# DeltaNet level: joining 32x32 block inverses with float32 products in place of zero-padded float16 operands

## The chip, the cores and the metric

The kernel runs on one core of one Trainium2 chip. Times are device microseconds of one execution of the whole program. The time before is 3229.03 us, the median of three runs (3227.76 to 3230.68). A profile is one execution of its own: the one read here took 3223.55 us, and its span from the first to the last instruction is 3221.8 us.

## The reference, cut to what matters

The layer normalises its input (two sequences of 4096 and 2048 rows, 1024 wide), projects it once, and runs three head groups on the projection: windowed attention, a gated DeltaNet in both directions of time, and cross-attention to a memory. Their gated outputs go through one output projection and a second layer norm. The part that the change touches is the triangular solve inside the DeltaNet, done for chunks of 64 rows, per head and per direction:

```python
a = jnp.einsum('...id,...jd->...ij', k_beta, k) * decay
def solve(rhs):
    return lax.linalg.triangular_solve(a, rhs, left_side=True, lower=True, unit_diagonal=True)
u = solve(v * beta[..., None])
w = solve(k_beta * jnp.exp(g)[..., None])
```

The unit triangular 64x64 matrix of a chunk is inverted by blocks. With the inverses A and B of its two 32x32 diagonal blocks and the 32x32 block N that lies off the diagonal, the missing block of the inverse is the product of three: A, N and B, with a sign. Joining the two inverses by these two small products is what the kernel calls a level.

## The kernel before, in words

A tile is 128 rows of a sequence, so it holds two chunks; there are 48 tiles and four DeltaNet heads. The program has three stages one after another. The first normalises, projects, convolves and does the windowed attention. The second goes forward over the 24 pairs of tiles: DeltaNet in the forward direction, with the gate projections and the memory attention (`gate_mem`, L1661) of the tiles as other work beside it. The third goes backward over the pairs: DeltaNet in the other direction, with the output projection and the last layer norm (`finish`, L1750) beside it. The loop of the second and third stage is `pipe` (L1705).

DeltaNet has these steps for each tile. `dn_front` (L1435) builds the decayed key products `n` for two pairs of tiles at a time and inverts their 32x32 diagonal blocks on GpSimd (`dn_invert`, L916: buffers `na`, `nb`, `tb`, with round trips through DRAM); the inverses come back as the tile `uc`, 128 partitions by 4 heads by 32 columns of float32. `dn_back` (L1455) then calls `dn_level` (L966), which joins the inverses to 64x64 ones in `th`, and `dn_chain` (L1011), which carries the state from tile to tile; its products with `th` (`psx`) and with `n` (`psb`) are float32 products of 64x64 blocks already.

The level before works with float16 pairs. `split` (L808) writes a float32 value as a high part (ScalarE, a copy to float16) and a low part (VectorE, the remainder), and `mm3` (L839) multiplies two such pairs with three matmuls. For a level `uc` is split into `tc_`, and VectorE transposes both parts in blocks of 32x32 into `tt`. The off-diagonal blocks of `n`, one for each of the two chunks (q = 0, 1), are split into `n64h` and `n64l`. These two, and `yth` and `ytl` for the second product, are 128x128 operands per head that are zero outside the two blocks; they exist once for the whole program (`dn_alloc`, L854) and were set to zero at the start of stages two and three (`dn_static`, L858). So each product handles all 128 partitions, and one matmul does both chunks.

The order of the instructions is not that of the code. Every call is recorded, and a planner (`schedule`, L342, and `order`, L268) simulates the engines with an estimated cost per instruction (`full_cost`, L137) and issues all of them in the order that it finds (`flush`, L500). On that account the profile puts nearly every instruction on L505, and instructions are told apart by the names of the tiles. For the PE the planner counts a matmul of n columns as the larger of 25 ns and n/2.4 ns plus 2.5 ns, four times that for float32. Each engine then runs its own list strictly in that order. The PSUM tiles of the level (`psy`, `psz`) share two buffers with the output of the chain (`pso`, tag "dn").

Of the kernel before, what the change touches and what calls it, by code (L numbers as in the profile page):

```python
# [9 lines left out]
F32 = mybir.dt.float32  # L10
F16 = mybir.dt.float16
BF16 = mybir.dt.bfloat16
I32 = mybir.dt.int32
AF = mybir.ActivationFunctionType
# [5 lines left out]
P = 128  # L20
# [530 lines left out]
def encoder(ctx: ExitStack, tc: tile.TileContext, A, outs):  # L551
    nc = tc.nc
    plan = Plan(tc)
    V, S, G, T, Q = plan.engines()
# [253 lines left out]
    def split(eng_hi, dst_h, dst_l, src, scale=None):  # L808

        if scale is None:  # L810
            S.activation(dst_h, src, AF.Copy)
            V.tensor_tensor(dst_l, src, dst_h, op=ALU.subtract)
        else:
            S.activation(dst_h, src, AF.Copy, scale=scale)
            V.scalar_tensor_tensor(dst_l, src, scale, dst_h, op0=ALU.mult, op1=ALU.subtract)
# [23 lines left out]
    def mm3(out, stat, mov, start=True, stop=True):  # L839

        T.matmul(out, lhsT=stat[0], rhs=mov[0], start=start, stop=False)
        T.matmul(out, lhsT=stat[0], rhs=mov[1], start=False, stop=False)
        T.matmul(out, lhsT=stat[1], rhs=mov[0], start=False, stop=stop)
# [3 lines left out]
    YB = 1  # L847
    NAB = 1
    KSB = 1
    dstat = {}  # L850
    for nm in ("n64h", "n64l", "yth", "ytl"):
        dstat[nm, 0] = [P, 4, 128]

    def dn_alloc(pool):  # L854
        for (nm, pr), shp in list(dstat.items()):
            dstat[nm, pr] = pool.tile(shp, F16, name=f"{nm}{pr}", tag=f"{nm}{pr}", bufs=1)

    def dn_static(dr):  # L858
        for s_ in dstat.values():
            V.memset(s_, 0.0)  # L860

    def features(pool, t, tag):
        fm = pool.tile([P, 8, P], F16, tag=tag, name=tag, bufs=2)
        Q.dma_start_transpose(out=fm, in_=dst_d[t].rearrange("p h t s d -> p (h t s d)"))
        return fm
# [100 lines left out]
    def dn_level(pool, psp, dr, d):  # L966

        uc, n = d["uc"], d["n"]
        i0, i1 = (0, 1) if dr == 0 else (1, 0)
        nn = n.rearrange("q h (b c) -> q h b c", b=4)  # L970
        tc_ = pool.tile([P, 2, 4, 32], F16, tag="tc", name="tc_", bufs=2)
        split(None, tc_[:, 0], tc_[:, 1], uc)
        tt = pool.tile([P, 2, 4, 32], F16, tag="tt", name="tt", bufs=2)
        V.transpose(tt.rearrange("p a h c -> p (a h c)"), tc_.rearrange("p a h c -> p (a h c)"))
        n64 = (dstat["n64h", 0], dstat["n64l", 0])
        for q in range(2):
            r = slice(64 * q + 32 * i0, 64 * q + 32 * i0 + 32)
            c = slice(64 * q + 32 * i1, 64 * q + 32 * i1 + 32)
            split(None, n64[0][r, :, c], n64[1][r, :, c], nn[r, :, 2 * q + i1])
        psy = psp.tile([P, 512], F32, tag="dn", name="psy")  # L980
        py = psy[:, 0:128].rearrange("p (h c) -> p h c", h=4)
        for h in range(4):
            mm3(py[:, h], (n64[0][:, h], n64[1][:, h]), (tt[:, 0, h], tt[:, 1, h]))
        yt = (dstat["yth", 0], dstat["ytl", 0])
        for q in range(2):
            r = slice(64 * q + 32 * i1, 64 * q + 32 * i1 + 32)
            c = slice(64 * q + 32 * i0, 64 * q + 32 * i0 + 32)
            split(None, yt[0][r, :, c], yt[1][r, :, c], py[r])
        psz = psp.tile([P, 512], F32, tag="dn", name="psz")
        pz = psz[:, 0:128].rearrange("p (h c) -> p h c", h=4)  # L990
        for h in range(4):
            mm3(pz[:, h], (yt[0][:, h], yt[1][:, h]), (tc_[:, 0, h], tc_[:, 1, h]))
        th = pool.tile([P, 4, 64], F32, tag="th", name="th", bufs=2)
        S.activation(th[:, :, 0:32], uc, AF.Copy, scale=rowA)
        S.activation(th[:, :, 32:64], uc, AF.Copy, scale=rowB)
        for q in range(2):
            r = slice(64 * q + 32 * i0, 64 * q + 32 * i0 + 32)
            c = slice(32 * i1, 32 * i1 + 32)
            S.activation(th[r, :, c], pz[r], AF.Copy)
        d["th"] = th  # L1000

    state = {}
# [452 lines left out]
    def dn_back(pool, psp, dr, tiles, ds, emit_out):  # L1455
        for i, (t, d) in enumerate(zip(tiles, ds)):
            dn_level(pool, psp, dr, d)
            first = pos_of[t] == 0 if dr == 0 else pos_of[t] == lens[seq_of[t]] - 1
            if first:
                dn_reset(pool)  # L1460
            emit_out(t, *dn_chain(pool, psp, dr, d))
# [137 lines left out]
    pn = p23.enter_context(plan.pool(name="pn", bufs=1))  # L1599
    pd2 = p23.enter_context(plan.pool(name="pd2", bufs=2, space=PSUM))  # L1600
    pb = p23.enter_context(plan.pool(name="pb", bufs=1, side="right"))
    dn_alloc(pn)
    dn_static(0)
    vmts = {}

    def memory(t):
# [129 lines left out]
            Q.dma_start(out=w[:, c:c + 2], in_=wo_d[:, 4 * i + c:4 * i + c + 2])  # L1736
    Q.dma_start(out=grow, in_=A["ln_g"][0].partition_broadcast(P))
    Q.dma_start(out=brow, in_=A["ln_b"][0].partition_broadcast(P))
    dn_static(1)
    osum = {}  # L1740

    def out_b(t, po, eg):
# [74 lines left out]
```

## Time and profile before

| | |
|---|---|
| median of three runs | 3229.03 us |
| the profiled execution, its span | 3223.55 us, 3221.8 us |
| PE busy | 2833.5 us, 88% of the span |
| PE weight loads busy | 1889.5 us, 59% |
| VectorE (DVE) busy | 2652.9 us, 82% |
| ScalarE (ACT) busy | 2179.3 us, 68% |
| GpSimd (POOL) busy | 1765.8 us, 55% |

A busy share is the part of the span in which the engine had an instruction in it. Matmuls overlap each other in the array, so their durations (0.38 us for one of 512 columns) are longer than the distance at which they follow each other, and the distance is what a matmul costs the PE. The rows on which the prediction rests stand further down.

### The profile page before, as it was taken

How to read it: one execution, taken by the hardware profiler on the slowest of the kernel's cores; microseconds unless marked ns; L12 is line 12 of the kernel's file. 1: busy time of each engine (PE TensorE's matmuls, PEld its weight loads, DVE VectorE, ACT ScalarE, POOL GpSimd, SP SyncE). 2: the span in 40 equal slices, each digit the busy share in tenths (PEclk: the TensorE clock that was granted, in tenths of full speed). 3: DMA queues.
4: the chain of work that ended last, by engine and by line, in shares of the span. 5: the costliest groups of instructions: out<-in, count | busy, mean ns of one | idle time of the engine just before them, and what ended most of it. 6: DMA issues, size and time to landing. Idle time of an engine off the chain costs nothing.

```text
span 3221.8 us, 79556 instructions
## 1 busy us (share of the span) xinstructions
PE 2833.5 (88%) x28704; PEld 1889.5 (59%) x28704; DVE 2652.9 (82%) x6256; ACT 2179.3 (68%) x5623; POOL 1765.8 (55%) x2923
## 2 busy tenths in 40 slices
PE   5789887888988897778999999999998998898998
PEld 4666766667666675445565555665554554554544
DVE  8799877899999999678878787887778887887875
ACT  5677756777777776577777667776666666565543
POOL 5756444455565455535734253444538766867762
PEclk9899988999999998889999999999999999999999
DMA  7999999999999999899888887877798887777763
GB/s 220 260 228 233 221 225 229 240 236 214 228 210 226 207 227 254 206 224 197 189 182 203 188 200 160 174 175 164 159 218 209 195 189 183 190 185 178 187 170 114
DMA packets 1336900, 652.35 MB, mean 202 GB/s; under 512 B 1127728, under 2 KB 1261744, under 8 KB 1332280
## 3 DMA queue, kind: packets, MB, share of 16 engines
q1 hardware_dynamic: 1336504, 647.27, 87.5%
q8 instruction: 225, 3.69, 0.5%
q14 instruction: 171, 1.40, 0.1%
HBM read 227.54 MB, written 175.19 MB: 125 GB/s over the span
## 4 chain that ended last, share of the span: by engine, by line
PE 24%; DVE 24%; POOL 19%; DMA 13%; issue 8%; ACT 8%; SPq 3%; POOLq 0%; ACTq 0%; DVEq 0%
PE psg L505 8%; POOL nb L505 6%; POOL tb L505 5%; DVE acc L505 5%; PE pso L505 4%; PE psf L505 3%; SPq L505 3%; DMA apt<-aphl 3%; DVE lg L505 2%; DVE aphl L505 2%; PE psk L505 2%; DMA na<-nd 2%; PE psx L505 1%; ACT lg L505 1%; DMA uc<-ud 1%
## 5 line engine op out<-in xcount | busy, mean ns | idle before, releaser
L505 PEld LDWEIGHTS <-xT 128*128 128x128 f16 x5760 | 535.7, 99 | 381.4 <-issue 43.8
L505 PE MATMUL psf<-xT,w1f 128*128 128x256 f16 (+1 forms) x3600 | 443.2, 276 | 13.3 <-DVE vtm L505 7.8
L505 PE MATMUL psg<-w2a,xT 128*128 128x512 f16 (+1 forms) x2304 | 435.5, 330 | 6.4 <-DVE qtm L505 4.4
L505 PEld LDWEIGHTS <-w1f 128*128 128x128 f16 x3600 | 341.0, 101 | 56.6 <-DVE vtm L505 7.2
L505 POOL TENSOR_TENSOR nb<-nb,tb 128x30 f32<-128x30 f32 (+6 forms) x750 | 342.7, 457 | 48.7
L505 POOL TENSOR_TENSOR tb<-nb,na 128x30 f32<-128x30 f32 (+6 forms) x750 | 327.0, 436 | 48.4
L505 DVE SCALAR_TENSOR_TENSOR acc<-cb,cw,acc 128x256 f32<-128x256 f32 x576 | 326.1, 598 | 7.3 <-POOL cb L505 4.6
L505 ACT ACTIVATE lg<-lg,mx,scal 128x385 f32<-128x385 f32 (+1 forms) x384 | 263.8, 688 | 89.7 <-DVE mx L505 81.6
L505 PEld LDWEIGHTS <-yT 128*128 128x128 f16 x2304 | 201.2, 98 | 193.2 <-issue 9.9
L505 PE MATMUL pso<-w2b,yT 128*128 128x512 f16 x1152 | 297.4, 385 | 0.0
L505 PE MATMUL pso<-w2a,yT 128*128 128x512 f16 x1152 | 291.5, 381 | 1.4 <-DMA yT<-yhl 1.4
L505 PE MATMUL pslg<-kfm,qfm 128*128 128x128 f16 x2240 | 197.3, 230 | 108.3 <-DVE mx L505 105.1
L505 PEld LDWEIGHTS <-qfm 128*128 128x128 f16 x2624 | 201.4, 102 | 154.3 <-issue 127.3
L505 PE MATMUL psg<-w2b,xT 128*128 128x512 f16 x1152 | 290.2, 384 | 0.0
L505 PE MATMUL psq<-w1t,xT 128*128 128x512 f16 x1152 | 283.2, 383 | 2.5 <-ACT cb L505 2.5
L505 POOL TENSOR_TENSOR x<-x,grow 128x256 f32<-128x256 f32 x208 | 189.1, 925 | 128.9 <-ACT x L505 117.4
L505 DVE TENSOR_TENSOR aphl<-lg,aphl 128x768 f16<-128x768 f32 (+1 forms) x192 | 201.5, 1049 | 56.2 <-ACT aphl L505 56.0
L505 POOL TENSOR_TENSOR n<-raw 128x256 f32<-128x256 f16 x96 | 79.6, 840 | 245.6 <-DMA raw<-cfh 113.1
L505 DVE CUSTOM_DVE_ANT_0 lg<-pslg,bias 128x385 f32<-128x385 f32 (+1 forms) x384 | 195.2, 540 | 22.8 <-ACT oat L505 10.8
L505 POOL TENSOR_TENSOR x<-x,brow 128x256 f32<-128x256 f32 x208 | 193.9, 949 | 0.0
L505 ACT ACTIVATE aphl<-lg 128x768 f16<-128x768 f32 (+1 forms) x192 | 156.4, 815 | 17.8 <-DMA apt<-aphl 15.9
L505 PE MATMUL psk<-w1t,xT 128*128 128x272 f16 x1152 | 157.9, 284 | 9.3 <-DVE qktm L505 9.2
(921 smaller groups left out, 6865.9 us busy)
## 6 DMA issues: line engine op xcount, KB each, us to landing
x<-x SPq DMA_DIRECT2D x48, 512.0 KB, 4.0
xT<-xT SPq DMA_DIRECT2D x24, 1024.0 KB, 5.8
xT<-xT SPq DMA_DIRECT2D x48, 512.0 KB, 4.7
r<-x SPq DMA_DIRECT2D x48, 512.0 KB, 4.1
out_dram<-r SPq DMA_DIRECT2D x48, 512.0 KB, 3.7
cr<-crow SPq DMA_DIRECT2D x47, 512.0 KB, 4.8
yhl<-yhl SPq DMA_DIRECT2D x48, 384.0 KB, 3.2
x<-in_x_prompt_dram SPq DMA_DIRECT2D x32, 512.0 KB, 4.9
```

The lines of the kernel that those rows point to most:

```text
L505: getattr(self.eng[o["e"]], o["name"])(*o["args"], **o["kw"])
```

## The change

The level takes its operands as they are, in float32, and multiplies the 32x32 blocks where they lie. There is no split of `uc`, of `n` or of the intermediate product, and there are no operands padded with zeros. Each product is now one matmul per head and per chunk, on 32 partitions, in place of three per head on 128 partitions. The transpose reads `uc` itself (float32, 128 columns, where it was float16, 256 columns). The intermediate product goes from PSUM to the tile `yt` by ScalarE as float32; `yt` has two buffers where `yth` and `ytl` had one. The last copies into `th` are the same as before.

```diff
-    dstat = {}
-    for nm in ("n64h", "n64l", "yth", "ytl"):
-        dstat[nm, 0] = [P, 4, 128]
-    def dn_alloc(pool):
...
-    def dn_static(dr):
-        for s_ in dstat.values():
-            V.memset(s_, 0.0)
...
-        tc_ = pool.tile([P, 2, 4, 32], F16, tag="tc", name="tc_", bufs=2)
-        split(None, tc_[:, 0], tc_[:, 1], uc)
-        tt = pool.tile([P, 2, 4, 32], F16, tag="tt", name="tt", bufs=2)
-        V.transpose(tt.rearrange("p a h c -> p (a h c)"), tc_.rearrange("p a h c -> p (a h c)"))
-        n64 = (dstat["n64h", 0], dstat["n64l", 0])
-        for q in range(2):
-            r = slice(64 * q + 32 * i0, 64 * q + 32 * i0 + 32)
-            c = slice(64 * q + 32 * i1, 64 * q + 32 * i1 + 32)
-            split(None, n64[0][r, :, c], n64[1][r, :, c], nn[r, :, 2 * q + i1])
+        tt = pool.tile([P, 4, 32], F32, tag="tt", name="tt", bufs=2)
+        V.transpose(tt.rearrange("p h c -> p (h c)"), uc.rearrange("p h c -> p (h c)"))
+        rows = [[slice(64 * q + 32 * i, 64 * q + 32 * i + 32) for q in range(2)] for i in (i0, i1)]
         psy = psp.tile([P, 512], F32, tag="dn", name="psy")
         py = psy[:, 0:128].rearrange("p (h c) -> p h c", h=4)
         for h in range(4):
-            mm3(py[:, h], (n64[0][:, h], n64[1][:, h]), (tt[:, 0, h], tt[:, 1, h]))
-        yt = (dstat["yth", 0], dstat["ytl", 0])
+            for q in range(2):
+                T.matmul(py[rows[1][q], h], lhsT=nn[rows[0][q], h, 2 * q + i1], rhs=tt[rows[0][q], h],
+                         start=True, stop=True)
+        yt = pool.tile([P, 4, 32], F32, tag="yt", name="yt", bufs=2)
         for q in range(2):
-            r = slice(64 * q + 32 * i1, 64 * q + 32 * i1 + 32)
-            c = slice(64 * q + 32 * i0, 64 * q + 32 * i0 + 32)
-            split(None, yt[0][r, :, c], yt[1][r, :, c], py[r])
+            S.activation(yt[rows[1][q]], py[rows[1][q]], AF.Copy)
         psz = psp.tile([P, 512], F32, tag="dn", name="psz")
         pz = psz[:, 0:128].rearrange("p (h c) -> p h c", h=4)
         for h in range(4):
-            mm3(pz[:, h], (yt[0][:, h], yt[1][:, h]), (tc_[:, 0, h], tc_[:, 1, h]))
+            for q in range(2):
+                T.matmul(pz[rows[0][q], h], lhsT=yt[rows[1][q], h], rhs=uc[rows[1][q], h], start=True, stop=True)
...
-    dn_alloc(pn)
-    dn_static(0)
...
-    dn_static(1)
```

## Rows read from the trace of the kernel before

**Rows 1.** The page, its first part: busy time, share, instructions.
```profile
PE 2833.5 (88%) x28704; PEld 1889.5 (59%) x28704; DVE 2652.9 (82%) x6256; ACT 2179.3 (68%) x5623; POOL 1765.8 (55%) x2923
```

**Rows 2.** Busy time by stage: stretch, length, engines, granted clock, DMA share, GB/s.
```profile
0.00:1380.00 1380.00, 1147.77 (x12288) 880.25 (x12288) 1192.66 (x2834) 971.41 (x2287) 734.68 (x903) 0.94 1.00 227
1380.00:2322.00 942.00, 871.75 (x8989) 554.27 (x8990) 761.57 (x1813) 687.88 (x1900) 437.60 (x956) 0.97 0.83 186
2322.00:3222.00 900.00, 814.01 (x7429) 455.01 (x7426) 698.66 (x1610) 520.03 (x1437) 593.53 (x1065) 0.98 0.75 182
```

**Rows 3.** The chain that ended last, 3150 to 3222 us: start, length, what.
```profile
3181.19 31.34 PE pso L505 x155
```

**Rows 4.** Waits of the PE, 1380 to 3222 us: total us, times, longest.
```profile
PE psx L505 <- DVE v L505: 27.0, 41, 1.9
PE psy L505 <- DVE tt L505: 26.4, 12, 5.8
PE psr L505 <- DVE shl L505: 16.1, 23, 2.0
PE psy L505 <- DVE of L505: 10.6, 8, 2.1
...
PE psk L505 <- DVE p L505: 7.6, 7, 3.2
PE psr L505 <- ACT shl L505: 6.2, 8, 2.0
...
PE psz L505 <- DVE ytl L505: 2.1, 4, 0.8
```

**Rows 5.** Groups of PE instructions by shape, 1380 to 3222 us: count, busy, mean ns.
```profile
L505 PE MATMUL psx<-v,th 64*64 64x64 f32 x1536 | 132.3, 226 | 31.8 <-DVE v L505 27.0 <-DVE ost L505 2.2 <-ACT th L505 0.9
...
L505 PE MATMUL psy<-tt,n64h 128*128 128x32 f16 x768 | 44.7, 178 | 37.6 <-DVE tt L505 26.4 <-DVE of L505 10.6 <-DVE ofs L505 0.3
```

**Rows 6.** The PE in order of time: start, length to the last end, what.
```profile
1594.91 0.68 PE L505 MATMUL psx<-v,th 64*64 64x64 f32 x8
1595.51 0.21 PE L505 MATMUL psy<-tt,n64h 128*128 128x32 f16 x2
...
1595.83 1.02 PE L505 MATMUL psg<-w2a,xT 128*128 128x512 f16 x4
1596.78 0.68 PE L505 MATMUL psb<-v,n 64*64 64x64 f32 x8
...
1598.57 0.68 PE L505 MATMUL psx<-v,th 64*64 64x64 f32 x8
1599.18 0.21 PE L505 MATMUL psz<-tc__22114,yth 128*128 128x32 f16 x2
...
1599.49 1.67 PE L505 MATMUL psg<-w2b,xT 128*128 128x512 f16 x7
1601.00 0.19 PE L505 MATMUL pss<-rx,kc 128*128 128x64 f16 x1
```

**Rows 7.** The tile psx: ns shortest, median, longest; first and last start.
```profile
L505 PE MATMUL psx<-v,th x1536: 218/218/366, 1410.3 to 3181.0; 64*64 64x64 f32 x192
```

**Rows 8.** Tiles n64h, n64l, ytl, tt, uc: ns shortest, median, longest.
```profile
L505 ACT ACTIVATE n64h<-n x192: 292/306/311, 1380.9 to 3158.2; 32x128 f16<-32x128 f32 x192
L505 DVE TENSOR_TENSOR n64l<-n,n64h x192: 236/287/716, 1383.0 to 3159.2; 32x128 f16<-32x128 f32 x192
L505 DVE TENSOR_TENSOR ytl<-psy,yth x192: 268/286/299, 1394.0 to 3170.4; 32x128 f16<-32x128 f32 x192
L505 DVE STREAM_TRANSPOSE tt<-tc__21583 x1: 388/388/388, 1381.2 to 1381.2; 128x256 f16<-128x256 f16 x1
L505 DVE STREAM_TRANSPOSE tt<-tc__26088 x1: 430/430/430, 3152.1 to 3152.1; 128x256 f16<-128x256 f16 x1
L505 ACT ACTIVATE tc__21583<-uc x1: 310/310/310, 1380.4 to 1380.4; 128x128 f16<-128x128 f32 x1
L505 DVE TENSOR_TENSOR tc__21583<-uc,tc__21583 x1: 292/292/292, 1380.8 to 1380.8; 128x128 f16<-128x128 f32 x1
```

More of the change, by code (lines that the diff above doesn't have):

```diff
@@ L849, in encoder @@
     KSB = 1
-    dstat = {}
-    for nm in ("n64h", "n64l", "yth", "ytl"):
-        dstat[nm, 0] = [P, 4, 128]
-    def dn_alloc(pool):
-        for (nm, pr), shp in list(dstat.items()):
-            dstat[nm, pr] = pool.tile(shp, F16, name=f"{nm}{pr}", tag=f"{nm}{pr}", bufs=1)
-    def dn_static(dr):
-        for s_ in dstat.values():
-            V.memset(s_, 0.0)
     def features(pool, t, tag):
@@ L995, in dn_level @@
         S.activation(th[:, :, 32:64], uc, AF.Copy, scale=rowB)
[L996 to L999, printed above, removed]
+        for r in rows[0]:
+            S.activation(th[r, :, 32 * i1:32 * i1 + 32], pz[r], AF.Copy)
         d["th"] = th
```

## The prediction

> **What bounds the kernel now.** I read the busy shares first, then the same by stage, then the chain that ended last, then what the PE waits for, and last the PE instruction by instruction around a level. The reader is to see that the PE is the fullest engine of the whole program [rows 1], and that in the two stages which run levels (1380 to 2322 us forward, 2322 to 3222 us backward) it is busy 871.75 of 942 and 814.01 of 900 us, against 761.57 and 698.66 us for VectorE and 687.88 and 520.03 us for ScalarE [rows 2]. The PE's idle time there is 70 + 86 = 156 us in 1842. The granted clock is 0.97 and 0.98, so it is nearly always at the 2.4 GHz level and a level has little to win or lose there. How the kernel ends says the same: the longest piece of the last chain is 31.34 us of output-projection matmuls back to back, 155 of them [rows 3]. The recurrence is over by then and the PE is working off a backlog, so what the levels add to the PE's list comes out at the end, unless the PE idles less elsewhere. So the change is a trade: dearer or cheaper PE work, against PE stalls that other engines cause. The first stage holds no level and stays as it is.
>
> **The price of a product on the PE now.** Distances between starts count, not durations. The 12 float16 matmuls of `psy` start at 1595.51 and the next group at 1595.83: 0.32 us, 0.027 us each. Those of `psz` take 1599.18 to 1599.49, 0.31 us [rows 6]. They are of the same shape as the gate matmuls around them, and nothing is lost at either side. There are 96 levels with two products each, 192 products at 0.315 us.
>
> **The price of a float32 group.** The chain's `psx` and `psb` are four calls of 64x64 blocks each and show as 8 records; the 1536 records of `psx` are two for each of 96 x 2 x 4 calls [rows 5]. So one float32 matmul is two records, and a product of the changed level (4 heads x 2 chunks) is 16 records of 32 columns. What surrounds such a group: seven gate matmuls fill 1599.49 to 1601.00, 0.216 us each; the four ahead of `psb` should take 0.864 us from 1595.83, but `psb` starts after 0.95 us, so entering costs 0.09 us. The group's length is 0.68 us to its last end [rows 6], and one record takes 0.218 us [rows 7]; the last starts 0.46 us after the first, 0.066 us apart. From there to the next group's start (1595.51) it is 0.14 us, 0.07 more than a distance. So a group costs 0.16 us for changing over, and 0.066 us a record of 64 columns.
>
> A rule of the Trainium skill speaks against the change at this place: "TensorEngine Tiling (Array Packing)", Tiling Modes, Key Properties, says that going from one tiling of the array to another drains it. The trace agrees as far as it goes, with the 0.09 and 0.07 us above. By the rule each of the 192 products pays this, and by the rows as well.
>
> A record of 32 columns in float32 stands in no row. Bounds: not below the 0.027 us of the float16 matmuls of 32 columns if the array takes one after the other; not above the 0.066 us of the 64-column record, if the cost doesn't fall with the columns. Half the latter, 0.033 us, is what columns alone would give, it is near the lower row, and I take it. Then a product costs 16 x 0.033 + 0.16 = 0.69 us, 0.375 us more than now, and 192 of them 72 us. With 0.027 us it is 53 us, with 0.066 us 173 us. Below that lies only the case in which the two chunks of a head run at the same time (first rival): half of 0.033 us a record, 21 us.
>
> **What the other engines lose.** VectorE: 192 `n64l` at 0.287 us (55 us), 192 `ytl` at 0.286 us (55 us), 96 low parts of `uc` at 0.292 us (28 us); 138 us. The transposes take 0.388 to 0.430 us for 256 float16 columns [rows 8]; for 128 float32 columns I allow from the same down to half, so 0 to 20 us saved, and take 10. The eight memsets are under 3 us. In all about 148 us of the 1460 us that VectorE is busy in the two stages. ScalarE: 192 `n64h` at 0.306 us and 96 high parts at 0.310 us [rows 8], 89 us of 1208; the copies to `yth` remain as copies to `yt`. None of this counts by itself, as neither engine sets the end; it counts where the PE waits for them.
>
> **What the PE stalls lose.** `psy` waited 26.4 us for `tt` [rows 4]. Today `uc` passes ScalarE, VectorE, VectorE before the matmul, and every hop queues behind other work; afterwards the transpose reads `uc` directly. I take back 20 of the 26.4 us, and the 2.1 us for which `psz` waited for `ytl`. The 10.6 us in which `psy` waited for `of`, the reader of the output in PSUM, stay: `psy`, `psz` and `pso` still share two buffers. The chain's own waits for VectorE and ScalarE (`psx` for `v` 27.0, `psr` for `shl` 16.1 and 6.2, `psk` for `p` 7.6: 57 us [rows 4]) get shorter, because these engines' queues are emptier: VectorE's idle share goes from 0.21 to (1842 - 1312)/1842 = 0.29, more by two fifths. I take a third, 19 us, an estimate; the bounds are none and all of the 57 us, since an operand that is late by its own chain stays late. Together 41 us, between 15 and 86.
>
> What is late next: `yt` now comes by ScalarE alone, and the PE meets it or waits for it as it does for `yth`; the level's last copies into `th` are unchanged, so `psx` still queues behind them. The added PE work delays what stands behind it in the PE's list, gate and output matmuls for the most part, which nothing waits for soon. The planner counts the new matmuls at 100 ns a call by its formula, 0.8 us a product, close to my 0.69 us, so it will leave room for them; but all else is put in a new order too, and that moves single waits either way.
>
> **Sum.** 72 - 41 = 31 us more: 3223.55 + 31 = 3254.6 us for an execution like the profiled one. The median of the runs shown stands 5.5 us above it, so 3260 us. The chance I give this case, slower with records near half price, is 0.50; its own range is 3240 to 3295.
>
> **Rivals.**
> 1. The two chunks of a head overlap in the array. They lie on other rows and other columns of it (partitions 0 to 63 and 64 to 127) and alternate in the issue. The direct cost is then 21 us and the net 21 - 41 = -20 us: 3209 us. It decides from a record distance of 0.02 us down: there 16 x 0.02 + 0.16 - 0.315 = 0.165 us a product, 32 us in all, and the 41 us outweigh it by more than 6.5 us. For it: nothing else would use the idle quarters of the array. Against it: no float32 rows in the trace come closer than 0.066 us, though all of those sit on one and the same block of the array. Chance 0.17. The Trainium skill has this rule in "TensorE: Matmul & The Clock Gate", Part 3, Packing small matmuls: matmuls in different row and column groups start a few ns apart. "TensorEngine Tiling (Array Packing)", Gotcha 1, speaks against it here, since row tiles may not be in one PSUM bank at the same time and both chunks write into `psy`. No run here shows either.
> 2. The emptier queues of VectorE and ScalarE are worth more than I take: with nearly all of the 86 us, and 12 more from waits too small to be listed, 72 - 98 = -26 us, 3203 us. For it: over half of the PE's 156 us of idle time ends with one of these two engines. Against it: an engine with a fifth of its time free makes others wait mostly by order, not by load. Chance 0.12.
> 3. A record costs as much with 32 columns as with 64: 173 - 41 = +132 us, 3361 us. For it: the weight load ahead of each record may be what sets the 0.066 us, and it might have a fixed part. Chance 0.12.
> 4. It evens out: direct cost at its lower bound of 53 us, stalls shrinking by about 53 us. Within 0.2% (6.5 us), about what a measurement of this kernel can tell from no change. Chance 0.09.
>
> **How the numbers follow.** The predicted time is that of the likeliest case, 3260 us. Slower by over 0.2%: 0.50 + 0.12 = 0.62. Faster by over 0.2%: 0.17 + 0.12 = 0.29. Within: 0.09. The range 3198 to 3330 us takes in the likeliest case, the first, second and fourth rival's times, and the third's up to a record distance of some 0.055 us; about 0.1 is left above it and 0.07 below.
>
> **What would show it.** In the profile after: `psy` and `psz` as 16 float32 records of 32x32 each, 3072 in all, with a group taking about 0.6 us to the next start and 0.09 us lost ahead of it; under 0.4 us means the first rival, over 1.1 us the third. VectorE busy about 148 us less and ScalarE 89 us less, all after 1380 us. The row of `psy` waiting for `tt` down to some 6 us. The backlog of output matmuls at the end as long as now or longer. The prediction is wrong if the PE's idle time in the two stages falls by more than the groups add, or if the first stage's length changes.

## The result, and the profile after

The changed kernel takes 3318.73 us (median of four runs, 3312.04 to 3322.77) against 3228.4 us for the kernel before: a ratio of 1.0279, 95% interval 1.0257 to 1.0300. It is slower by 90 us. The forecast was slower by 31 us; the range, to 3330 us, holds the time, but the size is three times what was forecast.

The page's first part after, which answers to [rows 1]:

```profile
PE 2918.9 (88%) x29472; PEld 1912.9 (58%) x29472; DVE 2504.9 (76%) x5768; ACT 2100.1 (63%) x5335; POOL 1741.8 (53%) x2923
```

VectorE is busy 148 us less, just as forecast, ScalarE 79 us less (89 were forecast), and the PE 85 us more. By stage (stretch, length, busy time of PE, weight loads, VectorE, ScalarE, GpSimd, granted clock, DMA share, GB/s), against [rows 2]:

```profile
0.00:1380.00 1380.00, 1146.60 (x12288) 878.64 (x12288) 1191.20 (x2832) 970.82 (x2287) 730.53 (x903) 0.94 1.01 227
1380.00:2322.00 942.00, 871.79 (x9001) 539.78 (x9002) 660.84 (x1506) 619.88 (x1674) 416.71 (x932) 0.97 0.78 178
2322.00:3314.00 992.00, 900.51 (x8184) 494.44 (x8183) 652.89 (x1430) 509.41 (x1374) 594.53 (x1088) 0.95 0.71 173
```

The first stage is as it was. The matmuls of the level's first product (ns shortest, median, longest; first and last start), against [rows 7]; 1536 records are 16 for each of 96 products, as forecast:

```profile
L505 PE MATMUL psy<-tt,n x1536: 190/191/258, 1382.4 to 3247.4; 32*32 32x32 f32 x192
```

The PE in order of time (start, length to the last end, what), against [rows 6]; first a product that stayed whole, then one that the planner cut in three:

```profile
1600.48 0.41 PE L505 MATMUL pso<-shl,fmc 128*128 128x64 f16 x8
1600.81 0.44 PE L505 MATMUL psy<-tt,n 32*32 32x32 f32 x16
1601.18 0.61 PE L505 MATMUL psg<-w2a,xT 128*128 128x512 f16 x2
...
1613.69 0.25 PE L505 MATMUL psy<-tt,n 32*32 32x32 f32 x4
1613.87 0.52 PE L505 MATMUL psmo<-vmt,mpt 128*128 128x64 f16 x12
1614.32 0.24 PE L505 MATMUL psy<-tt,n 32*32 32x32 f32 x2
1614.50 0.68 PE L505 MATMUL psx<-v,th 64*64 64x64 f32 x8
1615.10 0.37 PE L505 MATMUL psy<-tt,n 32*32 32x32 f32 x10
1615.40 0.61 PE L505 MATMUL psg<-w2b,xT 128*128 128x512 f16 x2
```

The whole product takes 0.37 us to the next start, and its 16 records lie within 0.44 - 0.19 = 0.25 us, 0.017 us apart. Ahead of it the eight matmuls of `pso` need 8 x 0.029 = 0.23 us and have 0.33 us: going in costs 0.10 us. So a whole product costs 0.47 us, 0.15 us more than before and not the 0.375 us of the forecast. The product cut in three goes in and out three times. Over the whole trace 32x32 groups are entered 320 times, not 192 times.

The pieces also tell which records share the array. The two records of a call that stands alone (`x2`, 1614.32) end 0.24 us after the first start, the four of two calls (`x4`, 1613.69) after 0.25 us: a second call, on the other chunk, costs next to nothing beside the first. In the trace the four records start at 0, 6, 52 and 59 ns (medians of 37 such pieces), those of a lone call at 0 and 52 ns (70 pieces).

What the PE waits for from 1380 us on (total us, times, longest), against [rows 4]:

```profile
PE psx L505 <- DVE v L505: 25.7, 31, 2.3
PE psy L505 <- DVE tt L505: 22.1, 9, 5.0
PE psr L505 <- DVE shl L505: 21.2, 31, 3.1
...
PE psr L505 <- ACT shl L505: 10.8, 14, 2.0
```

The relief that the forecast counted on doesn't show in these waits: `psy` waits for `tt` nearly as before, and `psr` waits more. And the backlog at the end is longer, 43.42 us where [rows 3] had 31.34 (chain that ended last: start, length, what):

```profile
3261.31 43.42 PE pso L505 x211
```

The busy time doesn't tell idle moments of the PE from work well, since a matmul of 0.38 us covers a pause that is shorter. So I measured starts. From 1380 us on, each PE record's distance to the next start is taken apart: up to the distance at which such records follow each other undisturbed (0.216 us for 512 columns, 0.109 for 256, 0.029 for 64) it is work; where float16 and float32 meet, up to 0.093 us more (and 0.049 us for the first float32 record) is going over; the rest is idle time.

| kernel | work | going over | idle |
|---|---|---|---|
| before | 1545 us | 68 us | 218 us |
| changed | 1544 us | 116 us | 263 us |

The 92 us between the two profiled spans are 48 us of going over and 45 us of what the table calls idle. The first is the change's own price, smaller than the 72 us forecast. The second is not all waiting: it holds the time that PE work loses where the granted clock is down. One such stretch of the changed kernel (window with its granted clock, the last figure but two; then the PE in it):

```profile
2737.00:2746.00 9.00, 9.00 (x72) 4.94 (x72) 1.78 (x5) 3.58 (x12) 4.92 (x11) 0.50 0.33 107
2739.33 1.46 PE L505 MATMUL pso<-w2b,yT 128*128 128x512 f16 x3
```

Here the clock is at its 1.2 GHz level, and the PE is busy all the time. Three 512-column matmuls take 1.46 us to the last end, where at 2.4 GHz they take 2 x 0.216 + 0.38 = 0.81 us. By the clock records of the two traces the PE was at 1.2 GHz for 83 us after 1380 us before the change, and for 148 us after it. Of the idle time, 41 and 68 us fall in these stretches; at 2.4 GHz it is about 176 and 192 us. So of the 45 us some 27 belong to the lower clock, most of them slower work, and some 16 to 18 us are more waiting, where the forecast had 41 us less. The experiments are about the waiting. How long the clock is down differs from execution to execution: in the 54 executions of before that the experiments have, its mean was 0.952 to 0.963, 0.959 in the middle, and the profiled one, with 0.963, stands at their upper end; the four of the changed kernel had 0.950 to 0.955. Whether the change itself lowers it is not shown.

### The profile page after: what moved, and what is told of

Read it like the earlier page. It is cut to its first block, busy times and chain, and to the rows that moved or that the text cites. A ratio compares the mean times of both kernels' runs of the same rounds, so it can differ in the third digit from the quotient of the medians.

```text
span 3314.0 us, 80307 instructions
## 1 busy us (share of the span) xinstructions
PE 2918.9 (88%) x29472; PEld 1912.9 (58%) x29472; DVE 2504.9 (76%) x5768; ACT 2100.1 (63%) x5335; POOL 1741.8 (53%) x2923
## 4 chain that ended last, share of the span: by engine, by line
PE 25%; DVE 24%; POOL 16%; DMA 13%; issue 9%; ACT 8%; SPq 3%; POOLq 0%; ACTq 0%; DVEq 0%
PE psg L505 8%; POOL nb L505 5%; DVE acc L505 5%; POOL tb L505 5%; PE pso L505 4%; SPq L505 3%; PE psf L505 3%; DMA cr<-crow 3%; DVE lg L505 2%; DVE aphl L505 2%; PE psx L505 2%; DMA apt<-aphl 2%; ACT lg L505 2%; PE psk L505 1%; POOL x L505 1%
## 5 line engine op out<-in xcount | busy, mean ns | idle before, releaser
L505 PE MATMUL psg<-w2a,xT 128*128 128x512 f16 (+1 forms) x2304 | 451.9, 334 | 14.6 <-DVE qtm L505 13.2
L505 POOL TENSOR_TENSOR nb<-nb,tb 128x30 f32<-128x30 f32 (+6 forms) x750 | 329.2, 439 | 49.5
L505 POOL TENSOR_TENSOR tb<-nb,na 128x30 f32<-128x30 f32 (+6 forms) x750 | 320.3, 427 | 48.0
L505 PE MATMUL pso<-w2a,yT 128*128 128x512 f16 x1152 | 308.5, 397 | 2.8 <-DMA yT<-yhl 2.8
L505 ACT ACTIVATE v<-psx 64x256 f32<-64x256 f32 x192 | 72.3, 377 | 204.5 <-PE psx L505 195.6
```

Of the source, the lines that this page charges most:

```text
L505: getattr(self.eng[o["e"]], o["name"])(*o["args"], **o["kw"])
```

## The experiments

Ratios are to the kernel before, run on the same chip, with 95% intervals. The medians of before lay between 3228 and 3236 us from chip to chip.

**Whole products.** The planner takes the eight matmuls of a product as one piece; its price stays at 8 x 100 ns.

```diff
-        for h in range(4):
-            for q in range(2):
-                T.matmul(py[rows[1][q], h], lhsT=nn[rows[0][q], h, 2 * q + i1], rhs=tt[rows[0][q], h], ...)
+        T.unit([(py[rows[1][q], h], nn[rows[0][q], h, 2 * q + i1], tt[rows[0][q], h], True, True)
+                for h in range(4) for q in range(2)])
```

> The changed kernel, with the eight matmuls of each product issued as one piece: the planner may no longer put other matmuls between them. In the changed kernel's trace 32x32 float32 groups are entered 310 times from float16 or 64x64 work, not 192 times, since the planner splits them. Theory A (the time went into changing the array over, about 0.2 us for going in and out): 118 groups fewer, 24 us less, about 3295 us. Rival B (the time went into a new order and its waits, the PE's price is small): no difference beyond 10 us from 3319 us.

3309.98 us, 1.0244 (1.0203 to 1.0285). 192 groups in place of 320 leave 98 us of going over in place of 116, but idle time is 282 us. The loss shrinks by 0.35%, 11 us. Cutting the products up is not the main loss.

**No low parts.** Before, without the VectorE work of `n64l` and `ytl`.

```diff
-            split(None, n64[0][r, :, c], n64[1][r, :, c], nn[r, :, 2 * q + i1])
+            S.activation(n64[0][r, :, c], nn[r, :, 2 * q + i1], AF.Copy)
...
-            split(None, yt[0][r, :, c], yt[1][r, :, c], py[r])
+            S.activation(yt[0][r, :, c], py[r], AF.Copy)
```

> The kernel before without the low parts of n64 and of yt: they stay zero, so the products lack these terms and the output is less exact. VectorE loses 384 instructions, 110 us, and the PE's list stays as it is. What the prediction took for emptier queues: 20 to 40 us less than before, about 3200 us. Theory A (the end is set by PE work, and freeing VectorE is worth next to nothing): 3220 to 3235 us, no measurable change.

3234.78 us, 1.0016 (0.9998 to 1.0033). Its page, first part:

```profile
PE 2843.3 (88%) x28704; PEld 1896.8 (59%) x28704; DVE 2539.4 (79%) x5872; ACT 2173.7 (67%) x5623; POOL 1755.8 (54%) x2923
```

VectorE is busy 113 us less and nothing is gained. A relief of VectorE by three quarters of what the change brings was worth nothing at the end, in the order that the planner made of it. In the profiled execution the PE's idle time at 2.4 GHz is 164 us, 12 us less than before, and the part at 1.2 GHz 66 us, 25 us more.

**Blocks in float16.** Before, with its splits, but 24 float16 matmuls of 32x32 per product, in one piece.

```diff
-        for h in range(4):
-            mm3(py[:, h], (n64[0][:, h], n64[1][:, h]), (tt[:, 0, h], tt[:, 1, h]))
+        T.unit([(py[ro[1][q], h], n64[a][ro[0][q], h, ro[1][q]], tt[ro[0][q], b, h], a + b == 0, a == 1)
+                for h in range(4) for q in range(2) for a, b in ((0, 0), (0, 1), (1, 0))])
```

> The kernel before with all its splits, but each product taken in 32x32 blocks where they lie, in float16: 24 matmuls of 32x32 in one piece in place of 12 of 128x128. No float32 and no relief of VectorE or ScalarE. Theory A (the price is that of the block shape: going in and out of 32x32 costs 0.2 us): 192 groups at 0.2 us and 24 records, 0.3 to 0.5 us, in place of 0.315 us: 35 to 75 us slower, 3265 to 3305 us. Rival C (the price is that of float32, the shape costs nothing): within 10 us of before.

3284.04 us, 1.0163 (1.0131 to 1.0194). The PE in order of time, around one product:

```profile
1602.78 0.41 PE L514 MATMUL pso<-shl,fmc 128*128 128x64 f16 x8
1603.12 0.22 PE L512 MATMUL psy<-tt,n64h 32*32 32x32 f16 x4
...
1603.52 0.45 PE L514 MATMUL psg<-w2a,xT 128*128 128x512 f16 x1
```

Here too the eight `pso` have 0.34 us for 0.23: going in costs 0.1 us in float16 as in float32. So going over has its price from the block shape, not from float32. The time itself can't be put down to the shape, because the planner counts this product 0.6 us, and the next runs show what that does.

**Only the order.** Before, the same instructions; the planner alone is told another price for a matmul of the level.

```diff
-            return max(25.0, 0.4167 * n + 2.5) * (4 if mybir.dt.size(ins[0].dtype) == 4 else 1)
+            c = max(25.0, 0.4167 * n + 2.5) * (4 if mybir.dt.size(ins[0].dtype) == 4 else 1)
+            return 800.0 / 12 if o.tensor.name.startswith(("psy", "psz")) else c
```

> The kernel before with the same instructions, but the planner counts the level's matmuls as dear as in the changed kernel (0.8 us a product in place of 0.3 us), so that it makes another order. Theory A: the order alone is worth little, 3220 to 3245 us. Rival B (the new order is the loss): 3270 us or more.

3302.05 us, 1.0218 (1.0186 to 1.0249). The order alone, without any of the change's work, costs 70 us: rival B. The clock isn't the reason: the four runs had 0.956 to 0.960, those of before on the same chip 0.955 to 0.962. What its PE waits for from 1380 us on:

```profile
PE psx L506 <- DVE v L506: 33.5, 49, 2.9
PE psr L506 <- ACT shl L506: 24.7, 29, 3.0
PE psr L506 <- DVE shl L506: 22.9, 33, 1.9
```

The waits on the chain from tile to tile have grown: `psr` for `shl` from 22.3 us [rows 4] to 47.6 us, `psx` for `v` from 27.0 to 33.5 us. The PE's idle time at 2.4 GHz has grown from 176 to 243 us. Two rivals for the reason: a price far from the truth makes a worse order, or the order of before is simply a lucky one. The same edit with 312 and with 500 ns a product tells:

> The kernel before with the same instructions, and the planner counting a matmul of the level 26 ns in place of 25 ns, a change of no meaning that still makes another order. Theory P: 3220 to 3240 us. Theory L: 3245 us or more, as any other order than the one of before.

3240.3 us, 1.0014 (0.9995 to 1.0033): a new order by itself costs next to nothing (the PE's list does differ from that of before, from the first level on). This is one other order; that the time follows the price in the runs below speaks against the lucky order too.

> The kernel before with the same instructions, and the planner counting a product of the level 0.5 us in place of 0.3 us. At 0.8 us it took 3302 us. Theory P: between, 3245 to 3275 us. Theory L: unrelated to the price, 3240 to 3310 us, about as likely above 3280 us as below.

3253.82 us, 1.0060 (1.0039 to 1.0080). The time follows the price.

**The changed work at other prices.** Whole products again, with the price handed over:

```diff
-                for h in range(4) for q in range(2)])
+                for h in range(4) for q in range(2)], 450.0)
```

> The changed kernel with each product in one piece, and the planner told 0.45 us a product, about what the trace shows (0.09 us going in, 16 records in 0.25 us, 0.12 us to the next start), in place of its 0.8 us. Theory P (the planner's price for the level makes a worse order, and the loss is mostly that): at least 30 us less than the 3310 us of the same kernel at 0.8 us, 3240 to 3280 us. Theory L (the order of before is a lucky one, and any change of the planner's inputs costs 20 to 80 us at random): anything from 3250 to 3320 us. Theory A (PE price): 3300 to 3315 us.

3259.1 us, 1.0071 (1.0046 to 1.0097).

> As the run at 0.45 us, with 0.3 us a product, which is what the planner counts for the 12 float16 matmuls of before. Theory P: 3235 to 3275 us, the level's dearer product on the PE (192 x about 0.15 us, 29 us) less what the relief of VectorE gives. Theory L: 3250 to 3320 us. Theory A: 3300 to 3315 us.

3236.94 us, 1.0003 (0.9982 to 1.0023): at the price that the planner gave the old product, the change makes no difference that can be measured. Its granted clock is 0.952 over the span, lower than the 0.955 of the changed kernel and the 0.963 of the profiled run before, so the clock is not what separates it from the changed kernel.

**The changed kernel with the price alone changed,** products not in one piece:

```diff
+            c = max(25.0, 0.4167 * n + 2.5) * (4 if mybir.dt.size(ins[0].dtype) == 4 else 1)
+            return 300.0 / 8 if o.tensor.name.startswith(("psy", "psz")) else c
```

> The changed kernel itself, its products not in one piece, with one edit: the planner counts a call of psy or psz 37.5 ns (0.3 us a product) in place of 100 ns. Theory P: most of the 90 us comes back, 3230 to 3265 us; what it is slower than the same in one piece (3237 us) is the price of split groups, at most 24 us. Theory A: 3310 us or more.

3253.8 us, 1.0081 (1.0062 to 1.0101). Of the 90 us this one line gives back about 65. What is left against the whole products is 0.8%, 25 us. Its trace has 267 groups in place of 192 and some 14 us more of going over; the rest is not traced.

**The PE work alone.** The order of the run at 450 ns, each product's matmuls issued twice in its piece.

```diff
-                for h in range(4) for q in range(2)], 450.0)
+                for _ in range(2) for h in range(4) for q in range(2)], 450.0)
```

> The kernel that ran in 3259 us with the planner's price of 0.45 us a product, in the same order of instructions, with each product's eight matmuls issued twice in its piece (the second overwrites the first): 16 more records a product and no more going in and out. By the trace that is 0.25 us each, 48 us for 192. If every us of PE work comes out at the end, 3307 us. If the PE only catches up with waits that were there anyway, under 3285 us.

3271.97 us, 1.0140 (1.0117 to 1.0164). The PE in order of time:

```profile
1605.88 0.69 PE L513 MATMUL psy<-tt,n 32*32 32x32 f32 x32
1606.51 0.60 PE L515 MATMUL psg<-w2a,xT 128*128 128x512 f16 x2
```

0.63 us in place of 0.37, so 0.26 us more for each of 192, 50 us. Of these 13 us come out at the end by the medians, which are from two chips, and 22 us by the ratios to before: between a quarter and a half. By distances the work is 49 us more and the idle time 37 us less. But only 8 of the 37 us are waits at 2.4 GHz; the rest lies in stretches at 1.2 GHz, of which this execution has 95 us after 1380 us and the one at 450 ns 141 us. So a part of the added work did not come out, and it is not shown that waits took it up.

**Below the true price.** Whole products at 150 ns, before at 150 ns, and whole products at 50 ns.

> The changed kernel with each product in one piece and the planner told 0.15 us a product, a third of what it takes. At 0.8, 0.45 and 0.3 us it took 3310, 3259 and 3237 us. If an underestimate goes on helping: 3200 to 3225 us. If it is a match of price and truth that counts: above 3240 us again.

3215.53 us, 0.9949 (0.9930 to 0.9969).

> The kernel before with the same instructions, and the planner counting a product of the level 0.15 us in place of 0.3 us; it really takes 0.315 us. If the low price alone makes the gain of the changed kernel at 0.15 us (3216 us): about 3215 us here too, 15 to 25 us less than before. If the gain belongs to the float32 blocks, whose lighter load of VectorE the order can then use: 3225 to 3240 us.

3219.75 us, 0.9957 (0.9942 to 0.9972). So the gain below 0.3 us belongs to the price, not to the float32 blocks.

> The changed kernel with each product in one piece, and the planner told 0.05 us a product. From 0.8 to 0.15 us the time fell by 94 us, about 15 us for each 0.1 us. If that goes on: 3195 to 3210 us. If the trend ends near where the price is half the truth: 3210 to 3225 us.

3208.52 us, 0.9932 (0.9915 to 0.9949), the fastest of all runs and faster than both kernels; from 150 to 50 ns the intervals overlap.

**One level for a pair of tiles,** 16 calls in a piece, 96 products.

```diff
-        tt = pool.tile([P, 4, 32], F32, tag="tt", name="tt", bufs=2)
+        tt = pool.tile([P, 8, 32], F32, tag="tt", name="tt", bufs=2)
...
+        T.unit([(py[rows[1][q], h], nn[h // 4][rows[0][q], h % 4, 2 * q + i1], tt[rows[0][q], h], True, True)
+                for h in range(8) for q in range(2)], 450.0)
```

> The changed kernel with one level for both tiles of a pair: 96 products of 16 calls in one piece in place of 192 of 8, half as many transposes, copies and groups, and the planner told 0.45 us for such a product (it should take about 0.7 us). 96 times less going in and out at 0.2 us is 19 us, and ScalarE has 288 instructions fewer. Against the 3237 us of single tiles at 0.3 us: 3210 to 3235 us; if the second tile's level comes too early for the order of the chain, no better than 3240 us.

3230.48 us, 0.9994 (0.9977 to 1.0011).

> One level for both tiles of a pair, the planner told 0.2 us for a product of 16 calls in place of 0.45 us (3230 us). With the slope seen for single tiles, 15 us for 0.1 us and half as many products: about 19 us less, 3205 to 3220 us. If the pair version waits for its operands and not for the PE: within 8 us of 3230 us.

3213.05 us, 0.9947 (0.9930 to 0.9963). Half the groups leave 83 to 84 us of going over in place of 96 to 98, and the time is that of single tiles at 150 ns: nothing gained beyond the price.

All of it side by side, ratio to before by the planner's price of a product (of a single tile):

| price | old work | new work, in one piece | new work, cut up | idle time old / new in one piece |
|---|---|---|---|---|
| 0.05 us | | 0.9932 | | - / 188 us |
| 0.15 us | 0.9957 | 0.9949 | | 203 / 190 us |
| 0.30 us | 1 | 1.0003 | 1.0081 | 218 / 212 us |
| 0.45 us | | 1.0071 | | - / 231 us |
| 0.50 us | 1.0060 | | | 244 / - |
| 0.80 us | 1.0218 | 1.0244 | 1.0279 (the change) | 298 / 282 us |

In each row old work and new work in one piece lie within 0.3% of each other; down each column the time rises with the price, and the PE's idle time with it. At 2.4 GHz alone, so without what the lower clock costs, the idle time is 152, 176, 190 and 243 us with the old work (0.15, 0.3, 0.5, 0.8 us) and 139, 140, 143, 159 and 212 us with the new (0.05 to 0.8 us). It too follows the price, and at equal price it is 12 to 33 us less with the new work. Against that stand 32 to 35 us more of going over, and at 0.3 and 0.8 us also 25 and 14 us more in stretches at 1.2 GHz. These are single profiled executions.

## Why the prediction was wrong

The direction was right, but most of the loss came from a term that is not in the sum. Point by point:

- **The step that failed** is the one on the planner: that it counts "0.8 us a product, close to my 0.69 us, so it will leave room for them". The product really takes 0.47 us, and the price was no harmless estimate: 0.8 us in place of 0.3 us costs 70 us with the old instructions (1.0218), more than three quarters of the loss, and the PE's idle time at 2.4 GHz rises from 176 to 243 us in that run. It should have stood in the sum as a term and not as a remark.
- **The price of the float32 groups**, 72 us, was too high. 16 records lie 0.017 us apart, not 0.033 us: the mechanism of the first rival, the two chunks in the array at once, is there, below the 0.02 us from which it was to decide, and a whole product reaches the next start in 0.37 us, under the rival's 0.4 us. Its gain of 20 us did not come, nor did it at a price of 0.3 us (1.0003). The rule of the Trainium skill in "TensorE: Matmul & The Clock Gate", Part 3, Packing small matmuls, that matmuls in different row and column groups start a few ns apart, agrees with the 6 to 7 ns of this trace. The restriction in the Trainium skill's "TensorEngine Tiling (Array Packing)", Gotcha 1, that row tiles may not be in one PSUM bank at the same time, did not keep the starts of the two chunks apart here, although both write into one PSUM tile. Going over, taken at 0.16 us, is 0.2 us, and it was paid 320 times and not 192 times, which the forecast missed. Together 48 us by distances.
- **What the other engines lose** was right: 148 us forecast and measured for VectorE, 79 against 89 us for ScalarE.
- **What the stalls lose**, 41 us, did not appear in the result: `psy` waited 22.1 us for `tt` in place of 26.4, and the waiting at 2.4 GHz rose by some 16 us. The higher price may have hidden it: at equal price the PE idles 12 to 33 us less at 2.4 GHz with the new work. That this comes from emptier queues is not shown. 113 us less VectorE work in the kernel before were worth nothing at the end and 12 us of this idle time, and the old work at 312 ns, in another order and without any relief, has 10 us less as well.
- **The clock** stood at nothing in the sum ("a level has little to win or lose there"). The granted clock of the last stage is 0.95 in place of 0.98, and in the two profiled executions 68 us in place of 41 us of what the table calls idle lies in stretches at 1.2 GHz. How much of this is chance is open, as said above.
- **"What the levels add to the PE's list comes out at the end"** is true by a quarter to a half (13 to 22 of 50 us), in the one order in which it was measured. The backlog at the end misled: it shows that the last 30 us are PE work, not that the 1800 us ahead of it are.
- What stays open: which decision of the planner a high price spoils. It is shown that the PE's idle time follows the price and that the chain's waits grow; one reading is that the order counts on a PE that is busy for the planned time, and the real PE arrives early at operands that are not ready. That is argued, not shown. Why a price below the truth still helps isn't explained either.

At equal price the change is worth nothing that can be measured, if its products are kept whole: some waits fewer, against the going over and, in these executions, a lower clock. With its products cut up and the price at 0.3 us it is 26 us slower (1.0081), close to the 31 us of the forecast without a term for the planner. That is partly luck: in its profiled execution going over costs 47 us more than before, the waits at 2.4 GHz are 30 us fewer, and 22 us more lie in stretches at 1.2 GHz, for 72, 41 and nothing in the forecast.

## What to carry to other kernels

Where the order of instructions comes from a planner with a cost table, a change of operand type changes the table's entry and with it the whole order: work out what the planner will believe beside what the chip will do, and run the old instructions at the new price before judging the new ones. Small matmuls in another block shape cost about 0.1 us going in and 0.1 us going out, so keep them together in one piece. A busy share says which engine is fullest, but only distances between starts say how much of it is waiting, and only once the stretches at the lower clock are taken apart.

## What was not expected of the hardware

Records of 32x32 float32 matmuls start 0.017 us apart on average, closer than the 0.027 us of the float16 matmuls of 32 columns on the full array and a quarter of the 0.066 us of 64x64 float32 records. Two calls on different blocks take 0.25 us to their last end, one call alone 0.24 us. Going over to the 32x32 shape costs the same 0.1 us in float16 as in float32.
